# First norm's weights on transposed x, and low halves of weight panels made by ScalarE and an accumulating DMA

## The chip, the core and the metric

One core of a Trainium2 chip runs the kernel alone. The metric is the device time of one execution in microseconds (us), the median of several runs. The engines are TensorE (PE, with its weight loads as PEld), VectorE (DVE), ScalarE (ACT), GpSimd (POOL) and SyncE (SP); each takes its instructions in the order of its own queue. SP and ACT issue ordinary DMAs, POOL issues the accumulating ones, which add what they read to what lies in the destination.

## The reference

Two layers over x of 512 tokens by 1024, all in float32. What matters here are the first norm, the projection `w_in`, and the projection `w_out`:

```python
for l in range(DEPTH):                       # 2 layers
    h = rmsnorm(x, norm1_g[l])               # x * rsqrt(mean(x^2) + eps) * norm1_g
    u = jnp.einsum('btd,de->bte', h, w_in[l])    # 1024 -> 3592 columns
    ...                                      # mLSTM, differential attention, HGRN2
    x = x + jnp.einsum('bte,ed->btd', mix, w_out[l])   # 1024 -> 1024
    h2 = rmsnorm(x, norm2_g[l])
    a = jnp.square(jax.nn.relu(jnp.einsum('btd,df->btf', h2, w_up[l])))
    x = x + jnp.einsum('btf,fd->btd', a, w_down[l])
```

The row scale of the norm (the rsqrt) is put on the results of the projection. The weights `norm1_g` go along the contracted dimension, so they can stand on the rows of `w_in` or on the columns of x.

## The kernel before, in words

To keep float32 accuracy each operand of a large product is split into a high half, rounded to fp32r, and a low half, the rest. A product is three matmuls per contracted tile: high by high, high by low, low by high (`nat_mm`, lines 294 to 296, with tokens as output rows; `t_mm`, lines 301 to 303, with output columns as rows).

Weights come in panels of 512 KB. All panels of the program stand in one list, `jobs`, each with its source, its width, its `gain` and the function that multiplies it. The loop at the end of the program prepares the panel of job n+2 (`AHEAD = 2`) and then runs job n. `panel` (line 265 on) loads the panel into `wraw` (a ring of 2 buffers, issued by SP at line 277), makes the high half `whi` on ACT and the low half `wlo` on DVE (rings of 3 each). So the high half of panel n+2 can be written once PE is done with panel n-1.

There are two ways to make the halves. Without a gain, `halves` (lines 239 to 243): ACT copies 512 columns at a time (L242), DVE subtracts (L243). With a gain, ACT multiplies each k tile by a column of `gcol`, the norm's weights turned onto partitions (L285), and DVE does multiply and subtract in one instruction (L286).

Each layer has 28 panels of `w_in` (with gain) and 8 of `w_out` (without), so 72 in the program. The order of the work in a layer: norm1 (`split_T`, line 333 on: four PE transposes of a 128x512 piece of x into PSUM, ACT makes the high half L340, DVE the low half L341), the `w_in` panels with HGRN, attention and mLSTM between them, the `w_out` panels, norm2, and then 16 groups of `w_up` and `w_down` panels. `block_panel` (line 245 on), for `w_up`, already adds blocks of weights with accumulating DMAs from POOL (L261); these land in `kT` and `mA`, not in the rings of halves.

`load_gains` (line 228 on) fetches the norms' weights, transposes them on PE (L234) and copies them to `gcol` (DVE L236). Across engines a tile scheduler sets the order of instructions; pieces marked `high_priority`, the panels and the splits among them, are drawn forward.

Of the kernel before, what the change touches and what calls it, by code (L numbers as in the profile page):

```python
# [8 lines left out]
F32 = mybir.dt.float32  # L9
F32R = mybir.dt.float32r  # L10
U8 = mybir.dt.uint8
AF = mybir.ActivationFunctionType
ALU = mybir.AluOpType
AX = mybir.AxisListType

P = 128
# [3 lines left out]
KT = D // P  # L20
# [41 lines left out]
def hybrid_kernel(ctx, tc, x, norm1_g, w_in, conv_w, gate_b, mlstm_g, qn_g, kn_g, lam_v, subln_g,  # L62
                  lb_param, hgrn_g, w_out, norm2_g, w_up, w_down, cst, msk, out):
    nc = tc.nc
# [13 lines left out]
    act = nc.scalar.activation  # L78
    V = nc.vector
# [146 lines left out]
    gcols = {}  # L226
# [38 lines left out]
    def panel(src, n, gain, prio=None, queue=nc.sync):  # L265


        w = src.shape[0] // P * n
# [7 lines left out]
        with tc.high_priority(prio):  # L276
            queue.dma_start(out=v3(raw), in_=src.rearrange("(k p) n -> p k n", p=P))
            if gain is None:
                halves(hi, lo, raw, w)
            else:  # L280
                l, c0 = gain
                for k in range(w // n):
                    ch = slice(k * n, (k + 1) * n)
                    g = gcols[l][:, c0 + k:c0 + k + 1]
                    act(hi[:, ch], raw[:, ch], AF.Copy, scale=g)  # L285
                    V.scalar_tensor_tensor(lo[:, ch], raw[:, ch], g, hi[:, ch].bitcast(F32),  # L286
                                           op0=ALU.mult, op1=ALU.subtract)
# [44 lines left out]

    def split_T(i, hh, hl, a, z=None):

# [3 lines left out]
        pv = pt.rearrange("p (k t) -> p k t", k=4)  # L338
        dh = hh[a][:, :, i * P:(i + 1) * P]
        nc.scalar.copy(dh, pv)  # L340
        V.tensor_sub(hl[a][:, :, i * P:(i + 1) * P], pv, dh.bitcast(F32))  # L341
# [414 lines left out]
    def add_layer(l):  # L756
# [7 lines left out]
        def norm1(i, cols):  # L764
# [8 lines left out]
            with tc.high_priority():  # L773
                split_T(i, S["hh"], S["hl"], a)

# [57 lines left out]
        def nat_group(c0, n, evac, first=None, after=None):  # L833
# [3 lines left out]
            for a in range(npan):  # L837
                def go(w, a=a):
# [9 lines left out]
                    if a == npan - 1 and after:  # L848
                        after()
                jobs.append((w_in[l, a * kk * P:(a + 1) * kk * P, c0:c0 + n], n, (l, a * kk), go))  # L850

        def t_group(w, g0, c0, hs, evac, halves=1, after=None):

            pts = {}
            for a in range(2):
                def go(wt, a=a):
# [10 lines left out]
                    if a == 1 and after:  # L867
                        after()
                jobs.append((w[l, a * 512:(a + 1) * 512, c0:c0 + 256], 256, (l, g0 + 4 * a), go))

        def t_panel(c0, evac, after=None):
            t_group(w_in, 0, c0, lambda: (S["hh"], S["hl"]), evac, 1, after)

# [86 lines left out]
        def nat_rows(w, r0, st, done):  # L960
# [16 lines left out]
            for c0 in (0, 512):  # L977
                jobs.append((w[l, r0:r0 + 256, c0:c0 + 512], 512, None, go))

        def nat_pair(w, r0, nk, st, n, add, done):  # L980

            kk = 1024 // n
            for c0 in range(0, D, n):
                pts = {}
                for a in range(0, nk, kk):
                    def go(wt, a=a, c0=c0, pts=pts):
                        for i in range(NT):
                            hi, lo = st(i)
                            for hf in range(n // 512):
# [5 lines left out]
                                if a + kk == nk:  # L995
# [3 lines left out]
                                    done(i, cols)  # L999
                    jobs.append((w[l, r0 + a * P:r0 + (a + kk) * P, c0:c0 + n], n, None, go))  # L1000

# [261 lines left out]
```

## Time and profile before

| | us |
|---|---|
| median of 3 runs (lowest, highest) | 1292.61 (1292.57, 1294.61) |
| the profiled execution | 1295.09 |
| its span, first to last instruction | 1293.3 |
| PE busy | 1276.0 (99%) |
| PEld busy | 1093.4 (85%) |
| DVE busy | 919.3 (71%) |
| ACT busy | 708.5 (55%) |
| POOL busy | 90.4 (7%) |
| DMA moved | 140.83 MB, 109 GB/s on the mean |

The shares of busy time are averages over stages. PE's busy time is that of pipelined matmuls with modelled ends, which overlap, so whether PE runs at its pace is read from the starts of matmuls that follow each other. Idle time of an engine that is not the bottleneck costs nothing.

### The profile page before, as it was taken

What the parts mean: (1) busy time and instruction counts of PE and PEld (TensorE: products, weight loads), DVE (VectorE), ACT (ScalarE), POOL (GpSimd) and SP (SyncE); (2) the same over time, 40 slices, a digit from 0 to 9 for tenths busy, and PEclk for the clock granted to TensorE, in tenths of its full rate; (3) what the DMA queues carried; (4) which work ended last, traced back from release to release, by engine and by line L of the source; (5) the groups of instructions that cost most, each with busy time, mean ns of one, the idle gap of its engine ahead of it and who ended that gap; (6) DMA issues with size and microseconds to landing.
All of it is one profiled execution on the core that took longest, in us unless ns stands there. A gap on an engine that the chain in (4) does not pass through costs nothing.

```text
span 1293.3 us, 20033 instructions
## 1 busy us (share of the span) xinstructions
PE 1276.0 (99%) x7492; PEld 1093.4 (85%) x7492; DVE 919.3 (71%) x2080; ACT 708.5 (55%) x1529; POOL 90.4 (7%) x92
## 2 busy tenths in 40 slices
PE   9999999999999999999999999999999999999998
PEld 6888777878999898989877887788788988888896
DVE  6786887977957566756557767878898666556663
ACT  6754874537644444544456457745386544444551
POOL 0000000000111011100000000000001111011100
PEclk9999999999999999999999999999999999999999
DMA  6222211224575576645332221112355675675452
GB/s 208 82 66 77 60 46 48 84 72 120 134 169 131 148 162 147 144 118 115 110 86 82 66 83 50 50 34 81 98 131 122 160 166 130 157 160 133 107 134 86
DMA packets 110229, 140.83 MB, mean 109 GB/s; under 512 B 5355, under 2 KB 79669, under 8 KB 110133
## 3 DMA queue, kind: packets, MB, share of 16 engines
q1 hardware_dynamic: 80228, 109.66, 27.6%
q0 software_dynamic: 29568, 29.36, 15.4%
q8 instruction: 59, 0.97, 0.3%
q10 hardware_dynamic: 336, 0.54, 0.1%
q14 instruction: 38, 0.30, 0.1%
HBM read 137.45 MB, written 2.10 MB: 108 GB/s over the span
## 4 chain that ended last, share of the span: by engine, by line
PE 90%; ACT 4%; DVE 4%; issue 1%; DMA 0%; POOL 0%; SPq 0%; DVEq 0%; ACTq 0%; POOLq 0%
PE pmm L294 16%; PE pmm L296 16%; PE pmm L295 15%; PE pmm L302 3%; PE pmm L303 3%; PE pmm L301 3%; PE pax L1132 3%; PE pax L1133 3%; PE pax L1131 3%; PE pax L686 2%; PE phx L1133 2%; PE ppv L1132 2%; PE phx L1131 2%; PE phx L1132 2%; PE ppv L1131 2%; PE ppv L1133 2%
## 5 line engine op out<-in xcount | busy, mean ns | idle before, releaser
L242 ACT CAST whi<-wraw 128x512 fp32r<-128x512 f32 x216 | 123.2, 617 | 185.8 <-PE pmm L296 141.6
L243 DVE TENSOR_TENSOR wlo<-wraw,whi 128x512 fp32r<-128x512 f32 x216 | 139.7, 685 | 76.0 <-ACT whi L242 75.9
L294 PE MATMUL pmm<-whi,h 128*128 128x512 f32 (+2 forms) x496 | 192.4, 388 | 0.0
L295 PE MATMUL pmm<-wlo,h 128*128 128x512 f32 (+2 forms) x496 | 190.2, 384 | 0.0
L296 PE MATMUL pmm<-whi,h 128*128 128x512 f32 (+2 forms) x464 | 177.7, 383 | 0.0
L285 ACT ACTIVATE whi<-wraw,gcol 128x256 fp32r<-128x256 f32 (+2 forms) x192 | 99.5, 572 | 79.2 <-PE pmm L296 61.2
L286 DVE SCALAR_TENSOR_TENSOR wlo<-wraw,gcol,whi 128x256 fp32r<-128x256 f32 (+2 forms) x192 | 101.8, 569 | 47.7 <-ACT whi L285 46.7
L1003 DVE TENSOR_TENSOR x<-x,pmm 128x512 f32<-128x512 f32 x144 | 98.6, 684 | 43.6 <-PE pmm L296 41.6
L294 PEld LDWEIGHTS pmm<-whi,h 128*128 128x128 f32 x496 | 93.7, 189 | 16.7 <-issue 0.2
L295 PEld LDWEIGHTS pmm<-wlo,h 128*128 128x128 f32 x496 | 93.7, 189 | 16.5 <-issue 0.2
L296 PEld LDWEIGHTS pmm<-whi,h 128*128 128x128 f32 x464 | 87.5, 189 | 16.6
L294 PE MATMUL pmm<-whi,yb 128*128 128x512 f32 (+2 forms) x256 | 100.5, 392 | 0.0
L295 PE MATMUL pmm<-wlo,yb 128*128 128x512 f32 (+2 forms) x256 | 98.6, 385 | 0.0
L295 PE MATMUL pmm<-wlo,ya 128*128 128x512 f32 (+2 forms) x240 | 92.0, 383 | 0.0
L294 PE MATMUL pmm<-whi,ya 128*128 128x512 f32 (+2 forms) x240 | 91.9, 383 | 0.0
L296 PE MATMUL pmm<-whi,yd 128*128 128x512 f32 (+2 forms) x224 | 86.0, 384 | 0.0
L296 PE MATMUL pmm<-whi,yc 128*128 128x512 f32 (+2 forms) x224 | 85.7, 383 | 0.0
L261 POOL DMA_DIRECT2D kT<-in_w_up_dram x42 | 56.0, 1334 | 394.4 <-DVE wlo L243 242.3
L242 ACT CAST whi<-kT 128x512 fp32r<-128x512 f32 x84 | 48.0, 619 | 61.5 <-PE pmm L296 30.7
L1131 PE MATMUL phx<-mid,whi 128*128 128x256 f32 x224 | 63.0, 281 | 0.0
L1132 PE MATMUL phx<-mid,whi 128*128 128x256 f32 x224 | 62.9, 281 | 0.0
L1133 PE MATMUL phx<-mid,wlo 128*128 128x256 f32 x224 | 62.9, 281 | 0.0
(466 smaller groups left out, 3311.5 us busy)
## 6 DMA issues: line engine op xcount, KB each, us to landing
wraw<-in_w_down_dram SPq DMA_DIRECT2D x64, 512.0 KB
wraw<-in_w_in_dram SPq DMA_DIRECT2D x51, 512.0 KB
kT<-in_w_up_dram POOLq DMA_DIRECT2D x42, 512.0 KB, 6.2
wraw<-in_w_up_dram SPq DMA_DIRECT2D x36, 512.0 KB
wraw<-in_w_out_dram SPq DMA_DIRECT2D x16, 512.0 KB
mA<-in_w_up_dram SPq DMA_DIRECT2D x14, 512.0 KB
kT<-in_w_up_dram SPq DMA_DIRECT2D x14, 512.0 KB
mA<-in_w_up_dram POOLq DMA_DIRECT2D x14, 512.0 KB, 6.1
```

The lines of the kernel that those rows point to most:

```text
L242: nc.scalar.copy(hi[:, ch], raw[:, ch])
L243: V.tensor_sub(lo[:, ch], raw[:, ch], hi[:, ch].bitcast(F32))
L261: nc.gpsimd.dma_start(out=v3(raw), in_=rows(b), accum_op=ALU.add)
L285: act(hi[:, ch], raw[:, ch], AF.Copy, scale=g)
L286: V.scalar_tensor_tensor(lo[:, ch], raw[:, ch], g, hi[:, ch].bitcast(F32), op0=ALU.mult, op1=ALU.subtract)
L294: mm(pt[:, :n], sh(a), wh[:, b], start=first and j == 0, stop=False)
L295: mm(pt[:, :n], sh(a), wl[:, b], start=False, stop=False)
L296: mm(pt[:, :n], sl(a), wh[:, b], start=False, stop=last and j == nk - 1)
L1003: V.tensor_add(xs[i][:, cols], xs[i][:, cols], pt)
L1131: mm(dst, wh[:, k, col], hh[:, k], start=k == 0, stop=False)
L1132: mm(dst, wh[:, k, col], hl[:, k], start=False, stop=False)
L1133: mm(dst, wl[:, k, col], hh[:, k], start=False, stop=k == 3)
```

## The change

The columns of x are multiplied by the first norm's weights while they are split (`split_T` with `gain`): eight instructions on 128 columns per piece, four on ACT and four on DVE, in place of one on each with 512. The `w_in` panels then need no gain. They and the `w_out` panels, all 72, get a third way to make halves (`gain == "dma"`): ACT copies the high half, ACT writes its negative into the low half, and POOL issues a DMA that adds the panel from DRAM a second time onto that. DVE has no part in it. `w_up`'s first panels keep the gain, `w_down`'s the subtraction.

```diff
             if gain is None:
                 halves(hi, lo, raw, w)
+            elif gain == "dma":
+                for a in range(0, w, w // 2):
+                    ch = slice(a, a + w // 2)
+                    nc.scalar.copy(hi[:, ch], raw[:, ch])
+                for a in range(0, w, w // 2):
+                    ch = slice(a, a + w // 2)
+                    act(lo[:, ch], hi[:, ch].bitcast(F32), AF.Copy, scale=-1.0)
+                nc.gpsimd.dma_start(out=v3(lo), in_=src.rearrange("(k p) n -> p k n", p=P), accum_op=ALU.add)
             else:
...
-    def split_T(i, hh, hl, a, z=None):
+    def split_T(i, hh, hl, a, z=None, gain=None):
...
+        if gain is not None:
+            for k in range(4):
+                g = gain[:, a * 4 + k:a * 4 + k + 1]
+                act(dh[:, k], pv[:, k], AF.Copy, scale=g)
+                V.scalar_tensor_tensor(hl[a][:, k, i * P:(i + 1) * P], pv[:, k], g, dh[:, k].bitcast(F32),
+                                       op0=ALU.mult, op1=ALU.subtract)
+            return
...
-                split_T(i, S["hh"], S["hl"], a)
+                split_T(i, S["hh"], S["hl"], a, None, gcols[l][:, 0:KT])
...
-                jobs.append((w_in[l, a * kk * P:(a + 1) * kk * P, c0:c0 + n], n, (l, a * kk), go))
+                jobs.append((w_in[l, a * kk * P:(a + 1) * kk * P, c0:c0 + n], n, "dma", go))
...
-                jobs.append((w[l, a * 512:(a + 1) * 512, c0:c0 + 256], 256, (l, g0 + 4 * a), go))
+                jobs.append((w[l, a * 512:(a + 1) * 512, c0:c0 + 256], 256,
+                             "dma" if g0 is None else (l, g0 + 4 * a), go))
...
-            t_group(w_in, 0, c0, lambda: (S["hh"], S["hl"]), evac, 1, after)
+            t_group(w_in, None, c0, lambda: (S["hh"], S["hl"]), evac, 1, after)
...
-                jobs.append((w[l, r0:r0 + 256, c0:c0 + 512], 512, None, go))
+                jobs.append((w[l, r0:r0 + 256, c0:c0 + 512], 512, "dma", go))
...
-                    jobs.append((w[l, r0 + a * P:r0 + (a + kk) * P, c0:c0 + n], n, None, go))
+                    jobs.append((w[l, r0 + a * P:r0 + (a + kk) * P, c0:c0 + n], n, "dma" if w is w_out else None, go))
```

The scheduler places instructions anew. Three places matter below.

ACT's queue at the start of the program, before. `x0_62` and `x1_63` are the first two token tiles of x, `pax_...` their transposes in PSUM, `h0_...` and `h1_...` the high halves of transposed x, `whi_6` the high half of the first weight panel, `whi_9` of the second:

```order
L317 ACTIVATE big_67,nss_22_131<-x0_62 128x512 x2
L340 CAST h0_18_127<-pax_25_134 128x4x128
L340 CAST h1_19_128<-pax_26_141 128x4x128
L285 ACTIVATE whi_6_85<-wraw_5_84,gcol_4_82 128x512 x2
L340 CAST h0_18_127<-pax_27_148 128x4x128
```

The same place now; `wlo_7` is the low half of the first panel:

```order
L283 CAST whi_6_85<-wraw_5_84 128x512
L351 ACTIVATE h0_18_130<-pax_25_137,gcol_4_82 128x128
L351 ACTIVATE h1_19_131<-pax_26_150,gcol_4_82 128x128
L283 CAST whi_6_85<-wraw_5_84 128x512
L351 ACTIVATE h0_18_130<-pax_25_137,gcol_4_82 128x128
L351 ACTIVATE h1_19_131<-pax_26_150,gcol_4_82 128x128
L283 CAST whi_9_95<-wraw_8_94 128x512
L286 ACTIVATE wlo_7_86<-whi_6_85 128x512
L283 CAST whi_9_95<-wraw_8_94 128x512
L351 ACTIVATE h0_18_130<-pax_25_137,gcol_4_82 128x128
L351 ACTIVATE h1_19_131<-pax_26_150,gcol_4_82 128x128
L286 ACTIVATE wlo_7_86<-whi_6_85 128x512
```

Just ahead of these rows stand the two squares of the first token tile, the first square of the second (`x1_63`), and two more L351. So from the first split of x to the second negated half of panel 1 there are eight L351 on 128 columns, four copies and two negations, behind a square that needs the second tile of x.

PE's queue at the same place, before:

```order
L234 MATMUL phx_3_80<-cst_66,r2_2_77 128x16
L337 MATMUL pax_27_148<-cst_66,x1_63 128x128 x4
L294 MATMUL pmm_48_236<-whi_6_85,h0_18_127 128x512
L337 MATMUL pax_28_155<-cst_66,x1_63 128x128 x4
L295 MATMUL pmm_48_236<-wlo_7_86,h0_18_127 128x512
L296 MATMUL pmm_48_236<-whi_6_85,h2_20_129 128x512
```

PE's queue there now:

```order
L234 MATMUL phx_3_80<-cst_66,r2_2_77 128x16
L302 MATMUL pmm_48_287<-whi_6_85,h0_18_130 128x512
L345 MATMUL pax_27_163<-cst_66,x1_63 128x128
L345 MATMUL pax_28_176<-cst_66,x1_63 128x128 x2
L345 MATMUL pax_27_163<-cst_66,x1_63 128x128
L345 MATMUL pax_28_176<-cst_66,x1_63 128x128
L345 MATMUL pax_27_163<-cst_66,x1_63 128x128
L345 MATMUL pax_28_176<-cst_66,x1_63 128x128
L345 MATMUL pax_27_163<-cst_66,x1_63 128x128
L302 MATMUL pmm_49_294<-whi_6_85,h0_18_130 128x512
L303 MATMUL pmm_48_287<-wlo_7_86,h0_18_130 128x512
L304 MATMUL pmm_48_287<-whi_6_85,h2_20_132 128x512
```

One matmul of the second token tile (`pmm_49`) now stands ahead of the first one that reads a low half (`wlo_7`); all the rest of PE's program stands behind that one.

POOL's queue in the first layer's `w_out` now. Before, the MEMSET and COPY rows alone stood here, in this order:

```order
L579 MEMSET mid_46_285 128x260
L287 DMA wlo_374_2414<-in_w_out_dram 128x2x512
L933 MEMSET yd_45_284 128x16
L287 DMA wlo_422_2695<-in_w_out_dram 128x2x512
L570 COPY mid_46_285<-big_67 64x1024 x2
L287 DMA wlo_429_2736<-in_w_out_dram 128x2x512
```

The accumulating DMAs share one queue with POOL's memsets and copies, which wait for other engines: `wlo_429`, a panel of `w_out`, is now behind the copies of the mLSTM keys (L555 before, L570 now), which wait for the convolution on DVE.

PE's queue at the end of the first layer's mLSTM, before. `kT_375` holds the halves of mLSTM's result, turned by the L744 transposes; `whi_445` and `whi_452` are the layer's last two `w_out` panels:

```order
L744 MATMUL phx_416_2637<-cst_66,big_67 128x128 x2
L294 MATMUL pmm_460_2911<-whi_445_2816,kT_375_2444 128x512
L295 MATMUL pmm_460_2911<-wlo_446_2817,kT_375_2444 128x512
L294 MATMUL pmm_469_2935<-whi_452_2852,kT_375_2444 128x512
L295 MATMUL pmm_469_2935<-wlo_453_2853,kT_375_2444 128x512
```

The same panels now; `whi_442` is the panel before them:

```order
L304 MATMUL pmm_450_2879<-whi_442_2813,mA_186_1271 128x512
L302 MATMUL pmm_460_2947<-whi_445_2850,kT_375_2474 128x512
L303 MATMUL pmm_460_2947<-wlo_446_2851,kT_375_2474 128x512
L304 MATMUL pmm_460_2947<-whi_445_2850,kT_375_2474 128x512
L302 MATMUL pmm_460_2947<-whi_445_2850,kT_375_2474 128x512
L303 MATMUL pmm_460_2947<-wlo_446_2851,kT_375_2474 128x512
L304 MATMUL pmm_460_2947<-whi_445_2850,kT_375_2474 128x512
L302 MATMUL pmm_469_2971<-whi_452_2887,kT_375_2474 128x512
L303 MATMUL pmm_469_2971<-wlo_453_2888,kT_375_2474 128x512
```

The transposes (L759 now) have moved 40 matmuls and more ahead, among those of the panel `whi_435` that comes before `whi_442`. Between the last use of `whi_435`, whose buffer `whi_452` takes, and the first use of `wlo_453` stand the 24 matmuls of `whi_442`, six of `whi_445` and one of `whi_452`.

## Rows read from the trace of the kernel before

**Rows 1.** Page: busy us by engine (section 1); the chain's shares (section 4).

```profile
PE 1276.0 (99%) x7492; PEld 1093.4 (85%) x7492; DVE 919.3 (71%) x2080; ACT 708.5 (55%) x1529; POOL 90.4 (7%) x92
PE 90%; ACT 4%; DVE 4%; issue 1%; DMA 0%; POOL 0%; SPq 0%; DVEq 0%; ACTq 0%; POOLq 0%
```

**Rows 2.** Timeline of PE at 606 us: start us, us, engine, line, instruction.

```profile
606.86 0.39 PE L295 MATMUL pmm<-wlo,h 128*128 128x512 f32 x1
607.08 0.40 PE L296 MATMUL pmm<-whi,h 128*128 128x512 f32 x1
```

**Rows 3.** Waits of PE's weight loads: in total us, times, longest us.

```profile
PEld phx L744 <- DVE big L632: 5.8, 2, 2.9
PEld pax L703 <- DVE mid L700: 3.1, 8, 0.7
PEld pax L686 <- DVE anm L687: 1.9, 8, 0.3
```

**Rows 4.** Groups by line and shape: count, busy us, mean ns, idle before.

```profile
L242 ACT CAST whi<-wraw 128x512 fp32r<-128x512 f32 x216 | 123.2, 617 | 185.8 <-PE pmm L296 141.6 <-PE pax L1132 21.9 <-PE phx L1132 15.9
L243 DVE TENSOR_TENSOR wlo<-wraw,whi 128x512 fp32r<-128x512 f32 x216 | 139.7, 685 | 76.0 <-ACT whi L242 75.9
L285 ACT ACTIVATE whi<-wraw,gcol 128x256 fp32r<-128x256 f32 x112 | 49.2, 499 | 32.6 <-PE pmm L296 18.4 <-PE pmm L302 12.2 <-DMA wraw<-in_w_up_dram 2.0
L285 ACT ACTIVATE whi<-wraw,gcol 128x512 fp32r<-128x512 f32 x64 | 43.3, 715 | 23.3 <-PE pmm L296 19.5 <-PE pmm L302 3.7
L286 DVE SCALAR_TENSOR_TENSOR wlo<-wraw,gcol,whi 128x512 fp32r<-128x512 f32 x64 | 45.7, 746 | 21.2 <-ACT whi L285 20.7
L286 DVE SCALAR_TENSOR_TENSOR wlo<-wraw,gcol,whi 128x256 fp32r<-128x256 f32 x112 | 49.1, 479 | 12.0 <-ACT whi L285 11.6
L340 ACT CAST h<-pax 128x512 fp32r<-128x512 f32 x16 | 9.2, 587 | 2.5 <-PE pax L337 2.0
L597 ACT ACTIVATE big<-big,mc 128x128 f32<-128x128 f32 x32 | 12.1, 395 | 6.4 <-PE ppv L611 3.3 <-DVE big L594 3.1
```

**Rows 5.** Accumulating DMAs, line L261: issue ns min/median/max; us to landing.

```profile
L261 POOL DMA_DIRECT2D kT<-in_w_up_dram x42: 1282/1282/1844, 313.8 to 1236.1; - x42
DMA to landing us min/median/max: 5.9/6.2/12.0
```

**Rows 6.** Timelines of ACT, DVE and PE at the start.

```profile
6.11 0.63 ACT L317 ACTIVATE big<-x 128x512 f32<-128x512 f32 x1 [1.49 <-DMA x<-in_x_dram]
8.14 0.17 DVE L236 COPY gcol<-phx 128x16 f32<-128x16 f32 x1 [1.06 <-PE phx L234]
9.12 1.09 PE L337 MATMUL pax<-cst,x 128*128 128x128 f32 x4 [1.02 <-DVE h L341]
11.14 0.78 PE L295 MATMUL pmm<-wlo,h 128*128 128x512 f32 x1
```

**Rows 7.** Timelines of ACT and PE: two panels, high half made, low half used.

```profile
49.98 1.32 ACT L285 ACTIVATE whi<-wraw,gcol 128x512 fp32r<-128x512 f32 x2
61.78 0.40 PE L295 MATMUL pmm<-wlo,h 128*128 128x512 f32 x1
...
923.96 1.14 ACT L242 CAST whi<-wraw 128x512 fp32r<-128x512 f32 x2 [1.94 <-PE pmm L296]
933.75 0.40 PE L295 MATMUL pmm<-wlo,kT 128*128 128x512 f32 x1
```

**Rows 8.** Timelines of POOL and PE round the mLSTM key copies.

```profile
254.22 2.13 POOL L555 COPY mid<-big 64x1024 f32<-64x1024 f32 x2 [13.59 <-DVE big L550]
262.61 0.47 PE L295 MATMUL pmm<-wlo,yb 128*128 128x512 f32 x1
```

**Rows 9.** Timeline of PE at the end of the first layer's mLSTM.

```profile
290.12 0.69 PE L744 MATMUL phx<-cst,big 128*128 128x128 f32 x2 [2.46 <-DVE big L632]
291.38 0.80 PE L294 MATMUL pmm<-whi,kT 128*128 128x512 f32 x1 [0.56 <-ACT kT L746]
```

**Rows 10.** Windows: us, busy of PE, PEld, DVE, ACT, POOL, PEclk, DMA share, GB/s.

```profile
290.00:296.00 6.00, 5.31 (x15) 3.93 (x16) 3.52 (x10) 1.37 (x3) 0.00 (x0) 0.50 0.67 231
```

## The prediction, made before the changed kernel was run

> **What bounds the kernel now.** I read the page's busy shares and its chain first [rows 1]: PE is busy 99% of the span and holds 90% of the chain, ACT and DVE 4% each. A busy PE need not be at its pace, so next comes its timeline in a steady stage [rows 2]: matmuls of 512 columns start 0.22 to 0.23 us apart, so the 24 of a panel take about 5.5 us. The reader is to see that the change can gain only where PE waits. The waits of its weight loads [rows 3] are small: 5.8 us at the end of mLSTM (two, one per layer), 3.1 and 1.9 us in attention, all on DVE. DVE's load of 919 us is therefore worth little by itself. Then I followed each panel from its high half on ACT to the first matmul that reads its low half [rows 7]; that lead decides whether a slower way to make low halves is seen.
>
> **What stays hidden.** DVE loses 160 multiply-and-subtracts of `w_in` and 32 subtractions on 512 columns [rows 4]: 28 panels in each of two layers are 56, 8 with two pieces of 512 give 32. ACT gains two negations for each of 72 panels, 144 × 0.617 = 89 us by the copy on as many elements [rows 4], less what plain copies save, and grows from 708 to about 785 us of 1293. POOL gains 72 issues at 1.28 us [rows 5], 92 us; the DMAs read 72 × 0.524 = 37.7 MB more on 140.8. None of the four gets near PE's 1276, so I price these at nothing, as long as each low half is there in time.
>
> **The price of a low half.** Before, it came some 0.7 us behind the high half. Now two copies (1.14 us together [rows 7]), two negations (as long), an issue and a landing must follow each other. The accumulating DMAs of `block_panel` move the same 512 KB onto 128 partitions: 5.9 us at least, 6.2 on the median, 12.0 at most [rows 5]. I take 6.2, so 1.14 to 1.25 + 0.2 + 6.2 = 7.6 us or a little more from the end of the copies to the use. The Trainium skill, "DMA: Bandwidth & Descriptors", section on the anatomy of one DMA on the SWDGE path, fits 2.0 us plus bytes over 436 thousand per us. By that 524,288 bytes would take an estimated 3.2 us, 3 us less than the row, and the sum below would be 3 us lower at the start; the row decides.
>
> **Part A, the start.** The norm's weights stand in `gcol` at 8.14 + 0.17 = 8.31 us [rows 6]. Before, x's first split did not need them; now ACT can't split until then. From there to the end of panel 1's negations its queue holds eight multiplications on 128 columns, four copies and two negations. Of a multiplication on 128 columns I have 0.395 us on another line, and 0.499 and 0.715 for 256 and 512 columns [rows 4], which extended gives 0.39 for one alone; following ones overlap a little (two copies take 1.14, not 2 × 0.617), so 0.35. Sum: 8 × 0.35 + 6 × 0.6 = 6.4, so 14.7; up to 1.5 more for the square of `x1` ahead, since that tile was there by 9.12 at the latest [rows 6]; I take 15.4. The landing makes it 21.6. In the trace the first low-half matmul began at 11.14 [rows 6]: a lag of 10.5 us. One matmul moved ahead of it takes 0.78 away. To that I add 1.0 for a longer time at half clock, since PE ran there at 0.78 us per matmul instead of the 0.40 of later ones, and 1.8 for panels 2 and 3 and the splits of `x2` and `x3`, which stand behind the waiting matmul. **A = +12.5**; below, with multiplications at 0.30, an early `x1` and nothing for the last two, +8; above, with a landing at 9.3 (half way from 6.2 to 12.0) and multiplications at 0.395, +17.
>
> **Part B, the split between the layers.** The same split stands at the end of layer 1: four multiplications at 0.35 instead of a copy at 0.587 on ACT [rows 4], and as many on DVE. Only the last piece is on the path, the others lie beside `w_down`'s matmuls. **+0.5**, between 0 and 1.5.
>
> **Part C, POOL's queue.** The DMA of `wlo_429` now stands behind the mLSTM key copies, which end at 254.22 + 2.13 = 256.35; with 6.2 it lands at 262.5, and its matmul came at 262.61 [rows 8]. It just fits; two layers, **+0.5**, between 0 and 3.
>
> **Part D, the end of mLSTM.** The L744 transposes have moved ahead past 40 matmuls and more, so their waits, 2.46 + 0.56 in layer 1 [rows 9] and in both layers about 7, can go; so can part of the half clock after them (PEclk 0.50 from 290 to 296 [rows 10]). What is late next is `whi_452`: from the release of its buffer to the use of its low half stand 31 matmuls, 31 × 0.23 = 7.1 us, and it needs 1.14 + 1.14 + 0.2 + 6.2 = 8.7: a new wait of 1.6 per layer, 3.2. Of the difference, −3.8, I take **−2**, since what the transposes wait for (L632 on DVE) is no earlier by itself. Bounds: −7 (the waits go and the new one doesn't come) and +3.
>
> **Part E, the steady panels.** Leads were 51.30 to 61.78, 10.5 us, in the run of `w_in` panels, and 8.65 at the smallest, 925.10 to 933.75 [rows 7]. Both are above 7.6: **0**. This cover is 1 us at the thinnest place and 2.5 to 3 elsewhere.
>
> **Sum.** 12.5 + 0.5 + 0.5 − 2 = +11.5. The profiled execution took 1295.09 (its span 1293.3 and what lies around it), 2.48 above the median of the runs; its sum gives 1306.6, the median 1292.61 + 11.5 = **1304.1 us**. With not all bounds at one end at once, this case lies from 1298 to 1312.
>
> **Rival 1, late landings in the steady stages (slower still).** Beside the weights' own loads the DMA share at 290 to 296 is 0.67 [rows 10], and the accumulating DMAs took up to 12.0 [rows 5]. If the usual landing is 9.3 instead of 6.2, a panel needs 1.14 + 1.14 + 0.2 + 9.3 = 11.8 from the release of its buffer to its use, and two panels and a matmul of PE's work give it 2 × 5.5 + 0.23 = 11.2. PE then waits about 0.6 us at each of some 25 panels that follow others without work between: +15, and A grows by 3 with its own landing. With 1304.1 that makes 1322, or **1320** with part D's gain kept whole. For it: 37.7 MB more, on the same queues as the loads. Against: the median of 42 such DMAs is near their minimum, though they too ran beside loads. It decides from a landing of 8.7 on.
> A rule speaks for this rival: by the Trainium skill, "SBUF — State Buffer", section on the two sides, a DMA issued by GpSimd can't have its descriptors written while DVE runs an instruction in a two-port mode. The 42 issues in this trace took 1282 ns and at most 1844 beside a busy DVE [rows 5], so at most 0.56 us would come of it.
>
> **Rival 2, faster: DVE's waits on PE's path go.** If the 111 us that DVE no longer works shorten its chains in attention and at the end of mLSTM, the 5.8 + 3.1 + 1.9 = 10.8 of [rows 3] go, and with the half clock of 290 to 296 [rows 10] (5.31 us of matmuls, half of it 2.7) 13.5 in all. Against A at its lower end, +8, that makes −5.5: about **1287**. It decides where A is under 13 and all these waits go. For it: each of these rows names DVE. Against: they are steps of chains in which each instruction waits for the one before, not work queued behind panels.
>
> **Rival 3, the start is paid back.** A at +8, the waits of D all gone (−7), B and C near nothing: about **1293**, no difference. Of the change not doing what it says I see no way: the rows of the order show DVE without panels of `w_in` and `w_out`.
>
> **How the numbers follow.** Forecast 0.60, rival 1 0.21, rival 2 0.10, rival 3 0.09. A measurement of this kernel tells 0.2%, 2.6 us, from no change. The first two are slower by more: 0.81; the second rival faster: 0.10; the third same: 0.09. The likeliest case gives 1304.1. A range from 1291 to 1322 takes in rival 3 and most of rival 1, and leaves out rival 2 and the far part of rival 1, some 0.17.
>
> **What would show it.** Right: PE's first low-half matmul begins near 21 us and waits for a DMA; a group of negations, 144 at about 0.6 us; 114 accumulating DMAs landing near 6.2; L759 without a long wait, and a wait of 1 to 2 us on a DMA at the last panel of `w_out`; no such wait in the run of `w_in` panels. Wrong: waits of PE on low halves of many panels (rival 1), a start under 8 us late, or attention's waits on DVE gone (rival 2).

## The result and the profile after

The changed kernel took **1302.53 us** (median of 6 runs, 1301.83 to 1303.13) against 1292.99 of the kernel before beside it: a ratio of 1.0074 (95% interval 1.0061 to 1.0087), 9.5 us slower. The forecast was 1304.1, 11.5 us slower. One run of the kernel before, at 1384.7 us, is 7% slower than its others and is left out of the ratio. The two profiled executions differ by less, 1300.8 - 1293.3 = 7.5 us of span; where the rest is turns up below.

The page of the changed kernel, busy times and the shares of the chain, against [rows 1]:

```profile
PE 1274.1 (98%) x7492; PEld 1091.5 (84%) x7492; DVE 834.7 (64%) x1936; ACT 768.7 (59%) x1673; POOL 178.9 (14%) x164
...
PE 86%; ACT 7%; DMA 2%; DVE 2%; issue 1%; SPq 0%; ACTq 0%
```

PE does the same 7492 matmuls in the same time; what it waits for has changed. DVE fell by 84.6 us, ACT rose by 60.2, POOL by 88.5, and the chain is now less on PE and more on ACT and DMA. The waits of PE's weight loads (total us, times, longest), against [rows 3]:

```profile
...
PEld pmm L303 <- DMA wlo<-in_w_in_dram: 6.6, 2, 5.3
PEld pmm L303 <- ACT big L325: 3.7, 2, 1.9
PEld pmm L302 <- ACT whi L283: 3.6, 1, 3.6
PEld pax L345 <- DVE h L352: 3.5, 1, 3.5
PEld pax L701 <- DVE anm L702: 2.6, 10, 0.3
PEld pax L718 <- DVE anm L702: 2.4, 10, 0.3
...
PEld pax L718 <- DVE mid L715: 1.5, 2, 0.8
```

L302 to L304 are the three matmuls L294 to L296 of before. The waits on mLSTM's transposes (L744, now L759) are gone, and waits on low halves `wlo` stand in their place. The second row is one of those too: it is the last `w_out` panel, where the profile names an ACT instruction; PE's own row for the same place names the DMA (further down). The new instructions, by line and shape (count, busy us, mean ns, idle before):

```profile
L286 ACT ACTIVATE wlo<-whi 128x512 fp32r<-128x512 f32 x136 | 80.2, 628 | 0.0
L283 ACT CAST whi<-wraw 128x512 fp32r<-128x512 f32 x136 | 78.5, 621 | 62.8 <-PE pmm L304 48.7 <-PE pmm L310 13.6
...
L287 POOL DMA_DIRECT2D wlo<-in_w_in_dram x56 | 69.5, 1247 | 348.8 <-ACT wlo L286 212.5 <-ACT rt L143 27.6 <-ACT h L351 20.5
...
L351 ACT ACTIVATE h<-pax,gcol 128x128 fp32r<-128x128 f32 x32 | 10.4, 375 | 7.2 <-PE pax L345 6.5 <-DVE h L352 0.7
...
L352 DVE SCALAR_TENSOR_TENSOR h<-pax,gcol,h 128x128 fp32r<-128x128 f32 x32 | 9.9, 346 | 8.4 <-ACT h L351 8.4
```

A negation on 512 columns costs 628 ns, as the copy does (621). The other 8 of the 144 negations have 528 columns; of L351 and L352, 64 each, half are shown, and the others write the halves of x into `ya`, `yb` and their like. The issues on the page, with the median us from issue to landing:

```profile
wlo<-in_w_in_dram POOLq DMA_DIRECT2D x52, 512.0 KB, 6.3
...
wlo<-in_w_out_dram POOLq DMA_DIRECT2D x16, 512.0 KB, 6.2
```

With 4 more for `w_in` these are the 72 new ones. The page has 42 into `kT` and 14 into `mA` besides, so 128 accumulating DMAs in all, not the 114 among the prediction's signs.

**The start.** PE's timeline (start us, us, line, instruction, idle before and what ended it):

```profile
10.15 0.80 PE L302 MATMUL pmm<-whi,h 128*128 128x512 f32 x1 [3.47 <-ACT whi L283]
13.92 2.01 PE L345 MATMUL pax<-cst,x 128*128 128x128 f32 x8 [2.97 <-DVE h L352]
17.15 0.79 PE L302 MATMUL pmm<-whi,h 128*128 128x512 f32 x1 [1.23 <-ACT h L351]
22.69 0.80 PE L303 MATMUL pmm<-wlo,h 128*128 128x512 f32 x1 [4.75 <-DMA wlo<-in_w_in_dram]
```

The first low-half matmul is at 22.69 instead of 11.14 [rows 6]. The chain behind it, on DVE, ACT and POOL:

```profile
6.72 0.17 DVE L236 COPY gcol<-phx 128x16 f32<-128x16 f32 x1 [0.23 <-PE phx L234]
8.36 0.63 ACT L325 ACTIVATE big<-x 128x512 f32<-128x512 f32 x1 [2.12 <-DMA x<-in_x_dram]
...
8.99 0.61 ACT L351 ACTIVATE h<-pax,gcol 128x128 fp32r<-128x128 f32 x2
...
13.59 1.71 ACT L286 ACTIVATE wlo<-whi 128x512 fp32r<-128x512 f32 x3
```

```profile
14.57 2.56 POOL L287 DMA_DIRECT2D wlo<-in_w_in_dram  x2 [10.94 <-ACT wlo L286]
17.92 1.20 POOL L287 DMA_DIRECT2D wlo<-in_w_in_dram  x1 [0.79 <-ACT h L351]
```

The norm's weights are in `gcol` at 6.89, and it isn't they that hold up the split: ACT begins to split x at 8.99, behind the square that waited for `x1`; the second negated half of panel 1 is the first of the three at 13.59; POOL issues at 14.57, and PE goes on at 22.69, 8.1 us later. Three such DMAs are under way together there, but that need not be what makes the landing long (the run with the first two panels by DVE, e3 below). For the eight issued from 10 to 60 us the view of `wlo` gives:

```profile
DMA to landing us min/median/max: 5.9/7.4/11.4
```

The windows of the start show the clock (the last three columns are the granted clock, the DMA share and GB/s):

```profile
5.00:10.00 5.00, 1.59 (x10) 0.88 (x8) 1.06 (x5) 2.37 (x8) 0.00 (x0) 0.87 1.03 406
10.00:15.00 5.00, 1.88 (x6) 1.30 (x7) 1.83 (x6) 5.00 (x14) 0.43 (x1) 0.50 0.68 189
15.00:20.00 5.00, 1.72 (x6) 0.81 (x4) 2.03 (x8) 5.00 (x17) 3.34 (x3) 0.50 0.95 193
20.00:25.00 5.00, 2.31 (x6) 1.83 (x7) 1.96 (x11) 2.23 (x10) 0.00 (x0) 0.50 1.06 218
25.00:30.00 5.00, 5.00 (x25) 4.03 (x24) 1.09 (x11) 1.38 (x6) 0.00 (x0) 0.92 0.87 153
```

With PE mostly waiting, the granted clock is 0.50, the lower of its two levels (1.2 GHz), from about 9 to 25 us.

**Where the time lies.** The panels are the same in every kernel here. The table has, for the first matmul on the low half of one panel, how many us later (or earlier, -) it starts than in the trace of before, read from PE's timelines; the columns are the times in the trace of before: the first panel, two of layer 1's `w_in` panels, layer 1's first `w_up` panel, two of layer 2's `w_in` panels, and the end of the span.

| kernel | 11.14 | 128.64 | 222.07 | 310.16 | 752.41 | 863.77 | 1293.3 |
|---|---|---|---|---|---|---|---|
| changed | 11.55 | 13.28 | 13.61 | 9.26 | 8.96 | 9.23 | 7.5 |
| e1_wout_only | -1.23 | -0.92 | -0.86 | -5.13 | -5.08 | -5.10 | -3.8 |
| e2_split_only | -0.64 | 6.16 | 6.12 | -0.24 | -0.65 | -0.71 | -4.5 |
| e3_first2_dve | -0.40 | 14.46 | 14.83 | 10.64 | 10.38 | 10.65 | 8.7 |
| e4_win_only | 9.90 | 13.31 | 13.71 | 7.45 | 7.17 | 7.43 | 3.6 |
| e6_first6_dve | -0.57 | 5.28 | 5.63 | -0.56 | -0.69 | -0.48 | -4.3 |
| e7_layer2_split | -0.85 | -1.13 | -1.11 | -3.70 | -4.08 | -4.19 | -8.0 |
| e8_no_weights | 11.96 | 10.38 | 10.75 | 4.68 | 4.70 | 4.95 | 1.1 |
| e9_pairs1_split2 | -1.32 | -1.74 | -1.72 | -7.44 | -7.83 | -7.92 | -11.8 |
| e11_pairs_only | -1.14 | -1.36 | -1.33 | -7.05 | -7.05 | -7.04 | -10.3 |

The start costs 13.3 us, the long run of `w_in` panels 0.3 more in each layer, the border of the layers -0.3, and each end of mLSTM gives back: 4.4 us in layer 1 (13.61 to 9.26), 1.7 in layer 2 (9.23 to 7.5). Kernels whose start is unchanged stand 0.9 to 1.7 us early there, so differences of about 1 us at the start mean nothing.

The end of mLSTM, where [rows 9] had the wait of 2.46; PE's timeline of the changed kernel:

```profile
290.76 0.38 PE L759 MATMUL phx<-cst,big 128*128 128x128 f32 x2
...
305.31 0.47 PE L303 MATMUL pmm<-wlo,kT 128*128 128x512 f32 x1 [1.39 <-DMA wlo<-in_w_out_dram]
```

```profile
942.73 0.47 PE L303 MATMUL pmm<-wlo,kT 128*128 128x512 f32 x1 [1.53 <-DMA wlo<-in_w_out_dram]
```

The transposes no longer wait, and the last panel's low half is late by 1.56 and 1.69 us (its start less the start before it and the 0.23 of a matmul).

A part of layer 1's 4.4 us is the clock. In the trace of before it was low from 290 to 296.5 (0.50 in [rows 10]), and in layer 2 at the same place it was 1.00. In e7, which keeps that place's order, the same wait of 2.46 us stands there, but the clock stays up:

```profile
289.00 0.44 PE L759 MATMUL phx<-cst,big 128*128 128x128 f32 x2 [2.46 <-DVE big L647]
```

```profile
291.00:293.00 2.00, 2.00 (x13) 1.63 (x13) 1.68 (x5) 0.99 (x3) 0.00 (x0) 1.00 0.87 288
293.00:296.00 3.00, 3.00 (x19) 2.34 (x18) 2.88 (x8) 2.59 (x7) 0.00 (x0) 1.00 0.00 1
```

and e7 gains 2.6 us there (-1.11 to -3.70) with nothing changed. So the profiled execution of before, 2.48 us above the median of its runs, holds a spell of low clock worth about 2.6 us. Without it the spans differ by 7.5 + 2.6 = 10.1, beside the 9.5 of the medians; the 1 us by which starts differ is as large as what is left.

### The profile page after: what moved, and what is told of

Its sections match the earlier page's. It is cut to its first block, busy times and chain, and to the rows that moved or that the text cites. A ratio compares the mean times of both kernels' runs of the same rounds, so it can differ in the third digit from the quotient of the medians.

```text
span 1300.8 us, 20189 instructions
## 1 busy us (share of the span) xinstructions
PE 1274.1 (98%) x7492; PEld 1091.5 (84%) x7492; DVE 834.7 (64%) x1936; ACT 768.7 (59%) x1673; POOL 178.9 (14%) x164
## 3 DMA queue, kind: packets, MB, share of 16 engines
q0 software_dynamic: 55296, 67.18, 35.2%
q1 hardware_dynamic: 80228, 109.66, 27.2%
## 4 chain that ended last, share of the span: by engine, by line
PE 86%; ACT 7%; DMA 2%; DVE 2%; issue 1%; SPq 0%; ACTq 0%
PE pmm L303 15%; PE pmm L304 15%; PE pmm L302 15%; PE pmm L310 3%; PE pmm L311 3%; PE pmm L309 3%; PE pax L1148 3%; PE pax L1147 3%; PE pax L1149 3%; PE pax L701 2%; PE phx L1149 2%; PE ppv L1148 2%; PE phx L1148 2%; PE phx L1147 2%; PE ppv L1147 2%; PE ppv L1149 2%
## 5 line engine op out<-in xcount | busy, mean ns | idle before, releaser
L242 ACT CAST whi<-wraw 128x512 fp32r<-128x512 f32 x184 | 104.9, 618 | 166.1 <-PE pmm L304 125.6
L302 PE MATMUL pmm<-whi,h 128*128 128x512 f32 (+2 forms) x496 | 191.3, 386 | 4.7 <-ACT whi L283 3.5
L304 PE MATMUL pmm<-whi,h 128*128 128x512 f32 (+2 forms) x464 | 178.0, 384 | 0.0
L243 DVE TENSOR_TENSOR wlo<-wraw,whi 128x512 fp32r<-128x512 f32 x184 | 118.8, 686 | 74.5 <-ACT whi L242 74.5
L283 ACT CAST whi<-wraw 128x512 fp32r<-128x512 f32 (+1 forms) x144 | 83.2, 621 | 83.3 <-PE pmm L304 69.3
L287 POOL DMA_DIRECT2D wlo<-in_w_in_dram x56 | 69.5, 1247 | 348.8 <-ACT wlo L286 212.5
L302 PEld LDWEIGHTS pmm<-whi,h 128*128 128x128 f32 x496 | 93.8, 189 | 21.5 <-ACT whi L283 3.6
L304 PEld LDWEIGHTS pmm<-whi,h 128*128 128x128 f32 x464 | 87.6, 189 | 16.6
L261 POOL DMA_DIRECT2D kT<-in_w_up_dram x42 | 56.0, 1336 | 325.6 <-DVE wlo L243 240.4
L302 PE MATMUL pmm<-whi,yb 128*128 128x512 f32 (+2 forms) x256 | 98.8, 386 | 0.0
L302 PE MATMUL pmm<-whi,ya 128*128 128x512 f32 (+2 forms) x240 | 92.3, 385 | 0.0
L304 PE MATMUL pmm<-whi,yd 128*128 128x512 f32 (+2 forms) x224 | 85.8, 383 | 0.0
L304 PE MATMUL pmm<-whi,yc 128*128 128x512 f32 (+2 forms) x224 | 85.7, 382 | 0.0
L286 ACT ACTIVATE wlo<-whi 128x512 fp32r<-128x512 f32 (+1 forms) x144 | 84.9, 628 | 0.0
```

What stands on the lines that cost most here:

```text
L242: nc.scalar.copy(hi[:, ch], raw[:, ch])
L243: V.tensor_sub(lo[:, ch], raw[:, ch], hi[:, ch].bitcast(F32))
L283: nc.scalar.copy(hi[:, ch], raw[:, ch])
L286: act(lo[:, ch], hi[:, ch].bitcast(F32), AF.Copy, scale=-1.0)
L287: nc.gpsimd.dma_start(out=v3(lo), in_=src.rearrange("(k p) n -> p k n", p=P), accum_op=ALU.add)
L302: mm(pt[:, :n], sh(a), wh[:, b], start=first and j == 0, stop=False)
```

## The experiments

Theory: the loss is the start, which the low halves by DMA and the weights on x share between them; the run of panels is covered; the end of mLSTM gives back. The main rival: the DMAs cost all along. Ratios are to the kernel before, beside which each ran.

**w_out's panels alone** (e1; the kernel before, with the DMA branch):

```diff
-                jobs.append((w[l, r0:r0 + 256, c0:c0 + 512], 512, None, go))
+                jobs.append((w[l, r0:r0 + 256, c0:c0 + 512], 512, "dma", go))
...
-                    jobs.append((w[l, r0 + a * P:r0 + (a + kk) * P, c0:c0 + n], n, None, go))
+                    jobs.append((w[l, r0 + a * P:r0 + (a + kk) * P, c0:c0 + n], n, "dma" if w is w_out else None, go))
```

> Only the 16 w_out panels get their low half from ACT and the accumulating DMA; the norm's weights stay on w_in's panels, which keep DVE. Theory (what the end of mLSTM gives back comes from w_out's low halves alone, and the start costs because of w_in's first panels): the order of the start is that of before, so no loss there; the transposes of the mLSTM result stand some 45 rows earlier in PE's queue, their waits on DVE (5.3 us of stalls before) and the stalls behind them (1.7) go, a wait of about 1.6 us per layer on the low half of the last w_out panel comes: -3.6 us, about 1289 against 1292.7, a ratio of 0.997. Rival (the gain at the end of mLSTM needs DVE free of w_in's panels too): no shift of those waits and two new ones of 1.6: 1296.

Measured: 1288.24 us, ratio 0.9946 (0.9928 to 0.9964). The start is unchanged, the L744 waits are gone, and the last panel waits 1.4 us in layer 1 and this in layer 2 (PE's timeline):

```profile
929.93 0.48 PE L303 MATMUL pmm<-wlo,kT 128*128 128x512 f32 x1 [2.87 <-DMA wlo<-in_w_out_dram]
930.24 0.49 PE L304 MATMUL pmm<-whi,kT 128*128 128x512 f32 x1
930.53 0.63 PE L302 MATMUL pmm<-whi,kT 128*128 128x512 f32 x1
930.96 0.63 PE L303 MATMUL pmm<-wlo,kT 128*128 128x512 f32 x1
```

Behind the wait the matmuls are 0.63 us long instead of 0.40. So in this execution layer 2 gains nothing (-5.10 to -3.8; the granted clock is 0.57 from 930 to 934), and layer 1 4.3 with the 2.6 of the clock in it. It is the slowest of the six, 1291.27 us, 3.0 above their median, so layer 2's loss is not that of the usual run.

**x's split alone** (e2), every panel with DVE's subtraction:

```diff
-                jobs.append((w_in[l, a * kk * P:(a + 1) * kk * P, c0:c0 + n], n, "dma", go))
+                jobs.append((w_in[l, a * kk * P:(a + 1) * kk * P, c0:c0 + n], n, None, go))
...
-                             "dma" if g0 is None else (l, g0 + 4 * a), go))
+                             None if g0 is None else (l, g0 + 4 * a), go))
```

(and w_out's two lines likewise)

> Only the first part of the change: x times the norm's weights while it is split; all 72 panels get their halves from an ACT copy and a DVE subtraction. Theory (the start's loss is mostly the low half's negations and landing, the smaller part the wait for the norm's weights and the splits in pieces of 128 columns): first low-half matmul near 15 to 16 us instead of 11.1 and 22.7; start +4 to +5, the end of mLSTM as before or a little better: about 1296, ratio 1.003. Rival (the split in small pieces and the wait for the weights make most of the loss): start +9 or more, 1302.

Measured: 1289.18 us, ratio 0.9954 (0.9937 to 0.997): faster than before, which neither side expected. The start is dearer by 6.1 us, but not at the first low half (which starts at 10.50, 0.64 us earlier): the clock is low until about 15, and later PE waits for a split, behind which the clock is 0.50 again from 29 to 32 (how the 6.1 add up from these is not worked out):

```profile
10.00:15.00 5.00, 5.00 (x14) 3.64 (x15) 4.74 (x17) 4.85 (x16) 0.00 (x0) 0.50 0.56 177
15.00:20.00 5.00, 4.77 (x22) 3.62 (x21) 3.86 (x15) 4.41 (x17) 0.00 (x0) 0.98 0.49 124
```

```profile
27.59 1.27 PE L345 MATMUL pax<-cst,x 128*128 128x128 f32 x8 [1.76 <-DVE h L352]
```

The surprise is the end of mLSTM, which gives back 6.4 (with the 2.6 of the clock) and 3.8 us with DVE as busy as before (912.2 us). So it needs neither low halves by DMA nor a DVE that is free. What moved is the order of PE's queue. DVE's last instruction before the transposes, L632 (now L647), first ended in layer 2 at 931.48 + 0.42 before. DVE's timelines, of before and of this kernel:

```profile
931.48 0.42 DVE L632 TENSOR_TENSOR big<-big,h 128x256 f32<-128x256 f32 x1
...
920.40 0.76 DVE L647 TENSOR_TENSOR big<-big,h 128x256 f32<-128x256 f32 x2
```

11 us earlier, with the panels of `w_in` 0.7 us early only. The scheduler has put mLSTM's matmuls ahead of `w_out` panels: layer 2's third `w_out` panel stands 8.7 us later than before, and the transposes find their input ready. The other kernels bear this out (the one with two DMAs per low half aside). Measured from the last `w_in` panel of the table in its layer, DVE's result comes 7.2 to 13.2 us earlier than before wherever the waits on these transposes are gone or under 0.3 us, and the third or fourth `w_out` panel comes 4.8 to 9.4 us later. In layer 1 of the kernel with the weights on x in layer 2 alone (e7, below) neither has moved, and the wait of 2.46 stands. Why the scheduler places them so is not shown.

**The first two panels by DVE** (e3), the rest as changed:

```diff
-        pend.append(panel(*jobs[n][:3], 0, (nc.scalar, nc.sync)[n]))
+        pend.append(panel(*jobs[n][:2], None, 0, (nc.scalar, nc.sync)[n]))
```

> The changed kernel, but the first two panels of the program get their low half from DVE instead of ACT and the DMA. Theory: the start's lag falls from about 13 us to 5 (the wait for the norm's weights and the small pieces stay), the end of mLSTM gives back 3.6 as in the changed kernel: about 1294, ratio 1.001. Rival (the start is slow since more bytes and the crowded POOL and ACT queues hold up every early panel): lag above 10 still, 1300 or more.

Measured: 1304.17 us, ratio 1.0067 (1.0048 to 1.0085): no better, the rival's number. PE's waits (total us, times, longest):

```profile
PE pmm L303 <- DMA wlo<-in_w_in_dram: 6.3, 2, 4.3
PE pmm L303 <- DMA wlo<-in_w_out_dram: 3.1, 2, 1.6
```

The wait of the start has only moved to the third panel (4.3 us) and the fourth (2.0). The timelines of POOL and PE have the third:

```profile
18.50 1.32 POOL L287 DMA_DIRECT2D wlo<-in_w_in_dram  x1 [14.87 <-ACT h L351]
27.50 0.51 PE L303 MATMUL pmm<-wlo,h 128*128 128x512 f32 x1 [4.28 <-DMA wlo<-in_w_in_dram]
```

It lands 9.0 us after its issue, though no other accumulating DMA is issued before 38.34; with 6.2 it would still have come too late, by 1.5 us. The fourth lands after 6.1 and is late all the same. So two things cost here, a short lead and a long landing at the start. What makes that landing long is open: the rival's crowded start is not excluded, three accumulating DMAs at once are not needed for it.

**w_in's panels alone by DMA** (e4; against the changed kernel):

```diff
-                jobs.append((w[l, r0:r0 + 256, c0:c0 + 512], 512, "dma", go))
+                jobs.append((w[l, r0:r0 + 256, c0:c0 + 512], 512, None, go))
...
-                    jobs.append((w[l, r0 + a * P:r0 + (a + kk) * P, c0:c0 + n], n, "dma" if w is w_out else None, go))
+                    jobs.append((w[l, r0 + a * P:r0 + (a + kk) * P, c0:c0 + n], n, None, go))
```

> The changed kernel with w_out's 16 panels back on DVE. Theory: the whole loss of the start (about 13 us) and none of what w_out's panels give back at the end of mLSTM: 1304 to 1306, ratio 1.009 to 1.010, 2 to 4 us slower than the changed kernel. Rival (DVE's relief by w_in's panels gives it back): 1302, as the changed kernel.

Measured: 1298.97 us, ratio 1.0034 (1.0021 to 1.0047), 3.6 us *better* than the changed kernel. The expected direction was wrong: the start costs its 13.3, and the ends of mLSTM give back 6.3 and 3.8, as in e2. Against this kernel the changed one loses 1.9 and 2.1 us at the two ends (4.35 against 6.26, and 1.7 against 3.8): the waits on its last `w_out` panels.

**The first six panels by DVE** (e6), the rest as e4:

```diff
-        pend.append(panel(*jobs[n][:3], 0, (nc.scalar, nc.sync)[n]))
+        pend.append(panel(*jobs[n][:2], None, 0, (nc.scalar, nc.sync)[n]))
...
-            pend.append(src() if callable(src) else panel(src, w, gain))
+            pend.append(src() if callable(src) else panel(src, w, None if n + AHEAD < 6 else gain))
```

> The kernel with DMA low halves for w_in and DVE for w_out (1299.0 us), but the first six panels of the program get their low half from DVE. Theory (the DMA's low halves cost only where the stream of panels starts, when nothing runs ahead yet; once panels follow each other every 5.5 us they are covered): the 7 to 8 us that this kernel has over the one with x's split alone go, 1289 to 1291, ratio 0.995 to 0.997. Rival (the first DMA panel, wherever it stands, pays its landing once): a new wait of 4 us or more at the seventh panel, 1294 to 1299.

Measured: 1290.63 us, ratio 0.9964 (0.9952 to 0.9976), as the theory has it. Its rows in the table lie within 1 us of e2's everywhere: 50 of `w_in`'s 56 panels with their low half by DMA cost some tenths of a microsecond in each layer (5.28 to 5.63 and -0.69 to -0.48, where e2 has 6.16 to 6.12 and -0.65 to -0.71) and bring nothing. The price of the DMA is paid where the stream of panels begins. That this is for want of a lead, and not for the crowd of transfers there, this run can't tell, since it also takes the first six DMAs out of the start.

**Two accumulating DMAs per low half** (e5):

```diff
-                    act(lo[:, ch], hi[:, ch].bitcast(F32), AF.Copy, scale=-1.0)
+                    act(lo[:, ch], hi[:, ch].bitcast(F32), AF.Copy, scale=-2.0)
                 nc.gpsimd.dma_start(out=v3(lo), in_=src.rearrange("(k p) n -> p k n", p=P), accum_op=ALU.add)
+                nc.gpsimd.dma_start(out=v3(lo), in_=src.rearrange("(k p) n -> p k n", p=P), accum_op=ALU.add)
```

> The changed kernel with every low half made as -2 times the high half plus two accumulating DMAs of the panel, one behind the other: low halves are doubled, so what comes out is not the reference's; only the time of landing is asked. Theory (the cover of a panel in the run is two panels and a matmul of PE, 11.2 us, against 8.7 needed): with a second issue and landing the need is 16 us, so panels that follow each other take 8.0 us instead of 5.5, on some 25 panels +62, the start +7, the last panels of w_out +7 each: near 1385. Rival (the cover is larger than that, since panels stand further apart than the ring shows): under 1330.

Measured: 1451.78 us (one run), 149 above the changed kernel where 83 were expected. PE's waits:

```profile
PE pmm L304 <- DMA wlo<-in_w_in_dram: 61.3, 22, 7.5
PE pmm L304 <- DMA wlo<-in_w_out_dram: 29.0, 10, 6.4
PE pmm L312 <- DMA wlo<-in_w_in_dram: 15.3, 6, 3.5
```

38 waits of 105.6 / 38 = 2.8 us, where some 25 of 2.5 were expected, and a granted clock of 0.957 on the mean, against 0.993. The waits are 105.6 of the 149 us; the rest is not split up, and the lower clock is in it. The size for a panel was right, and so was the cover: 11.2 us hold 8.7 and do not hold 16. The number of panels that follow closely was too low.

**Layer 2 alone with the weights on x** (e7), layer 1 as before, no DMA low halves:

```diff
-                split_T(i, S["hh"], S["hl"], a, None, gcols[l][:, 0:KT])
+                split_T(i, S["hh"], S["hl"], a, None, gcols[l][:, 0:KT] if l else None)
...
-                jobs.append((w_in[l, a * kk * P:(a + 1) * kk * P, c0:c0 + n], n, None, go))
+                jobs.append((w_in[l, a * kk * P:(a + 1) * kk * P, c0:c0 + n], n, None if l else (l, a * kk), go))
```

(against e2; the panels of `t_group` likewise)

> Layer 1 as in the kernel before (weights of the norm on w_in's panels, DVE's low halves), layer 2 with the weights on x and DVE's low halves; no DMA low halves at all. Theory (the split of x costs 6 us only at the program's start, and the weights on x move the end of mLSTM forward in its own layer, 4 us in each): start 0, first layer's end of mLSTM as before, the layers' border -0.4, second layer's end of mLSTM about -4: 1288 to 1290 against 1292.7, ratio 0.997. Rival (what the split gains in layer 2 comes from the later start of the whole program): no change, 1293.

Measured: 1287.86 us, ratio 0.9941 (0.9921 to 0.9961). The border of the layers gives 0.4, layer 2's end of mLSTM 3.8.

**DMA low halves for w_in, no weights on x** (e8; against e4):

```diff
-                split_T(i, S["hh"], S["hl"], a, None, gcols[l][:, 0:KT])
+                split_T(i, S["hh"], S["hl"], a)
```

> DMA low halves for w_in, DVE for w_out, and x split as before in one copy of 512 columns; the first norm's weights are left out altogether. Theory (the start's loss is a sum: 6 us for the weights on x, 7 for the DMA low halves): start +7 and the end of mLSTM -6 in the first layer and -4 in the second, as without the DMA: about 1290 to 1293. Rival A (the two losses lie on one chain, and the DMA low half is late only since ACT waits for the weights): start +2, 1286 to 1288. Rival B (the DMA alone makes the loss): start +12 or more, 1297.

Measured: 1297.47 us, ratio 1.0022 (1.0008 to 1.0036); rival B is nearest. PE's timeline:

```profile
23.09 0.79 PE L303 MATMUL pmm<-wlo,h 128*128 128x512 f32 x1 [8.61 <-DMA wlo<-in_w_in_dram]
```

The DMA alone makes 10.4 us of the start's 13.3, the weights alone 6.1 (e2); the two overlap by 3. ACT's copies of x stand ahead of the negations here too, and the DMA of panel 1 is issued at 14.71, as in the changed kernel (14.57): the second negation is late by its place in ACT's queue, not by the weights.

**Six w_out panels of each layer by DMA, the last two on DVE** (e11), w_in as before (against e1):

```diff
-                jobs.append((w[l, r0:r0 + 256, c0:c0 + 512], 512, "dma", go))
+                jobs.append((w[l, r0:r0 + 256, c0:c0 + 512], 512, None, go))
```

> The kernel before, with six of each layer's eight w_out panels by the DMA, the last two on DVE; the weights of the norm stay on w_in's panels. Theory (the waits of 1.4 and 3.0 us that the kernel with all w_out panels by DMA showed belong to the last panel's low half): both go, 3 to 4 us less than that kernel (1288.2): 1285 to 1286, ratio 0.993. Rival (what is late at that place is the result of mLSTM itself, so that the wait comes back under another name): 1288.

Measured: 1284.87 us, ratio 0.9927 (0.9914 to 0.9941). No wait on a low half is left, and layer 2's end of mLSTM now gives 3.3 us (-7.04 to -10.3).

**The best of both** (e9): those six panels in layer 1, the weights on x in layer 2 (against e7):

```diff
-                    jobs.append((w[l, r0 + a * P:r0 + (a + kk) * P, c0:c0 + n], n, None, go))
+                    jobs.append((w[l, r0 + a * P:r0 + (a + kk) * P, c0:c0 + n], n, "dma" if l == 0 and w is w_out else None, go))
```

> Layer 1 as before except that six of its eight w_out panels (not the last two, which are used first after the mLSTM transposes) get their low half by the DMA, which moves the transposes of the mLSTM result 45 rows forward; layer 2 with the weights on x and DVE's low halves. Theory (each of the two ends of mLSTM gives back its 3.4 us of stalls when its transposes stand later than DVE's result, by whatever edit, and the DMA's low half costs only on the last two panels): 3.4 us less than the kernel with layer 2 alone (1287.9), 1284 to 1285, ratio 0.992. Rival (the low halves by DMA are needed on the last panels for the gain, or another wait takes its place): 1287 to 1288, no gain over that kernel.

Measured: **1283.71 us**, ratio 0.992 (0.9905 to 0.9935): 9.6 us faster than before (1293.35 beside it), 18.8 below the changed kernel. Against e11 alone the step is 1.2 us. The longest waits of PE that are left:

```profile
PE ppv L114 <- DVE mpf L507: 1.5, 1, 1.5
PE pax L345 <- DVE h L356: 1.1, 1, 1.1
PE phx L413 <- DVE yb L419: 0.8, 1, 0.8
```

## Why the prediction was right, point by point

- **A, the start: +12.5 forecast, 13.3 measured**, and part of the closeness is luck. ACT's chain began where the sum had it, at 9.0, but behind the square of `x1` and not for the norm's weights, which were there at 6.89. It was shorter than forecast (issue at 14.57, the negations forecast to end at 15.4; a pair of multiplications on 128 columns took 0.61 us, not 2 × 0.35), and the landing was longer, 8.1 us instead of 6.2. PE began at 22.69, forecast 21.6. The 1.8 for later panels was spent: 1.03 us of it is a wait for the fourth panel's DMA, after 43.64. That the weights on x and the DMA stand one behind the other, as the sum had it, e2 and e8 show to be half right: they overlap by 3 us.
- **B, the border: +0.5 forecast, -0.3 measured** (9.26 to 8.96; e7 -0.4, e8 without the small pieces 0.0). My bound excluded a gain there without a reason; why the small pieces gain was not tried.
- **C, POOL's queue: +0.5 forecast, nothing seen.** The panel behind the key copies is used 22.1 us later than in the trace of before (284.70 instead of 262.61), since mLSTM's work moved ahead of it.
- **D, the end of mLSTM: -2 taken; about -3.5 measured without the clock** (4.4 + 1.7 less 2.6), beside the -3.8 that the sum had worked out. The new waits were forecast at 1.6 a layer and came at 1.56 and 1.69. The step that failed is the sentence for taking less, that "what the transposes wait for (L632 on DVE) is no earlier by itself". It is earlier, since PE's order feeds it earlier: L647 starts at 927.49 in layer 2, 4 us before L632 did (931.48), in a kernel whose panels run 9 us late. I had read the move of the transposes from the order, and not the move of the matmuls that feed DVE.
- **E, the steady panels: 0 forecast, 0.3 a layer measured**, which e6 has too and e2 has not. The cover is shown by e5, which goes past it.
- Sum: 13.3 + 0.3 (the run, twice, and the border) - 3.5 = 10.1, against 9.5 of the medians; forecast 11.5.
- **Rival 1** fell: landings in the run are 6.3 and 6.2 us on the median, and no long wait on a low half stands in the run of panels. That the new DMAs go "on the same queues as the loads" was misread: the page puts the accumulating ones on q0, 29.36 MB before and 67.18 now, and keeps 109.66 MB on q1. The Trainium skill, "SBUF — State Buffer", section on the two sides, says that GpSimd can't write a DMA's descriptors while DVE runs an instruction in a two-port mode; the eight issues from 10 to 60 us took 1203 to 1533 ns, so no more than 0.3 us of it shows there. By the Trainium skill, "DMA: Bandwidth & Descriptors", section on the anatomy of one DMA on the SWDGE path, 512 KB would take an estimated 3.2 us; no landing of the 72 was that short (5.6 at least), and the measurement decides.
- **Rival 2** was right in what would go and wrong in why: the waits at the end of mLSTM went, by order, not by a lighter DVE (84.6 us less, not the 111 that I had put). Attention's waits on DVE did not go: 1.5 of the 3.1 us on `mid` stayed, and on `anm` there are now 2.6 + 2.4 where 1.9 stood [rows 3].

## What to carry to other kernels

Moving work off an engine that is not the bound gained nothing by itself here; a slower way to make an operand is nearly free where a buffer's lead covers it (here 8.7 us needed, 11.2 given) and is paid where the stream begins and at the last panel before a turn of the dependence. Where a scheduler orders the queues, look for gains in what the edit moves: here any edit that put mLSTM's matmuls ahead of the `w_out` panels gave 3.1 to 3.9 us of stalls back in its layer, the expensive one and the free one alike, less what the last panels' low halves cost. Keep the old way for the first panels and for those used right behind a serial chain.

## What the runs showed of the hardware

- Accumulating DMAs of 512 KB land later near the start of the kernel: with three together the first was used 8.1 us after its issue, and the view from 10 to 60 us has 7.4 on the median and 11.4 at most, against 6.2 and 6.3 on the median of the whole run. In e3 a single one took 9.0 there, so it is not only their number.
- A wait of PE doesn't always bring the low clock: after the same wait of 2.46 us it was 0.50 in layer 1 of the trace of before, 1.00 in layer 2 of the same trace, and 1.00 in layer 1 of e7's, a difference of 2.6 us between executions with the same work.
- At the start of the kernel before the profile gives a granted clock of 1.00 from 9 to 13 us, though matmuls of 512 columns start 0.43 us apart there and 0.23 later; in the changed kernel the same spacing of 0.43 stands beside 0.50. What holds PE back in the former isn't settled. Behind the first low half that spacing lasts 2.7 us in the changed kernel (22.69 to 25.42) and 1.9 before (11.14 to 12.99), so the 1.0 us for it in part A was too much.
